# A hand-written engine order over five sub-layer boundaries, and adaLN weights loaded and multiplied in pairs

## The chip, the core and the metric

The kernel runs on one core of a Trainium2 chip. The metric is the device time of one launch, in microseconds (us). Engines are called TensorE (PE in the rows, PEld for its weight loads), VectorE (DVE), ScalarE (ACT), GpSimd (POOL) and SyncE (SP, whose queue issues nearly all DMAs).

## The reference, cut to what matters

Two layers of a hybrid trunk, for 128 context tokens (sample 0) and 128 latent tokens (sample 1), with the same weights and D = 1024. Everything is float32.

```python
def _layer(x, cond, st, l, p, alpha):
    ada = (silu(cond) @ p['w_ada'][l] + p['b_ada'][l]).reshape(..., 9, 1, D_MODEL)
    sh1, sc1, g1, sh2, sc2, g2, sh3, sc3, g3 = [ada[:, j] for j in range(9)]
    f1 = swiglu(x * (1 + sc1) + sh1, ffn1_w_gate, ffn1_w_up, ffn1_w_down)   # 1024 -> 2816 -> 1024
    x = layer_norm(alpha * x + 0.5 * g1 * f1, ...)
    y, new_st = mixer(x * (1 + sc2) + sh2, st, l, p)                        # GLA and mLSTM, merged
    x = layer_norm(alpha * x + g2 * y, ...)
    f2 = swiglu(x * (1 + sc3) + sh3, ffn2_w_gate, ffn2_w_up, ffn2_w_down)
    x = layer_norm(alpha * x + 0.5 * g3 * f2, ...)
```

So there are six sub-layers (FFN, mixer, FFN, twice) and five boundaries between them. At a boundary the LayerNorm of one sub-layer has to finish before the first product of the next can start.

## The kernel before, in words

Each weight matrix is cut into blocks of 512 output columns, and a block into units of up to four 128-row tiles. `load` fetches a unit from HBM in halves (`raw`, 512 KB, six buffers in `raw_p`), and `split_w` splits each half into a high part on ScalarE (`hi`, L304) and a low part on VectorE (`lo`, L305), seven buffers each. `consume(s, u)` multiplies unit u for sample s: per 128-row tile three matmuls, L320 (high x high), L321 and L322 (the cross terms), into the accumulator `acc0` or `acc1`. The main loop at the end of `hybrid_step` walks over all units: it consumes unit i for sample 0 and unit i-2 for sample 1 (LAG = 2).

The modulation values (adaLN) come from 9216 further weight columns a layer. `ada_unit(grp, k)` does one 128-row tile of two 1024-column pieces: two DMAs of 512 KB (`araw`), and four matmuls L168, each with 32 columns of weights in a column strip of its own of the array (`tile_position`), 512 moving columns and float32 operands; the profile has two records for each of these matmuls, since a float32 product takes two passes. 64 such products (the adaLN products of this text) are spread over the sub-layers by the list `due`; in the before version their weights come through `raw_p`.

At a boundary `ln_half` (VectorE: L378 or L380, L381, L382) takes half a row of the last product, `ln_finish` aggregates (L393), gets the reciprocal root through GpSimd (L386, L387), normalises `y` (L399), and `modulate` transposes it (L349, tile `xT`), applies scale and shift alternately on VectorE (L353) and ScalarE (L355) out of one PSUM bank, and splits the features into `xh` (ScalarE, L331) and `xl` (VectorE, L333). `residuals` then forms the next `x` (L420, L421).

In the mixers, `gates` and `chain` compute running maxima `Gr`, write them to DRAM (`Gd`, L589), and `rows_load` reads them back broadcast to all partitions (`Db`, L598); `decays` uses them on VectorE (L610).

What sets the order: a tile scheduler orders the instructions of every engine ahead of time from priorities, dependences and expected times; each engine then runs its list in order. Inside a `tc.manual_schedule` block the listed engines keep the order of the code. SP's queue also runs in order: an issue that waits holds up those behind it.

Of the kernel before, what the change touches and what calls it, by code (L numbers as in the profile page):

```python
# [28 lines left out]
LAG = 2  # L29
SLOTS = 21  # L30
PRIO = 100
# [3 lines left out]
def hybrid_step(ctx: ExitStack, tc: tile.TileContext, I, O, n_sub=6):  # L35
# [120 lines left out]
    def ada_unit(grp, k):  # L156

        raw = []
        for l, v in grp:
            r = raw_p.tile([128, 2, 512], F32, name="araw", tag="raw")  # L160
            nc.sync.dma_start(r.rearrange("p q n -> p (q n)"),
                              I["w_ada"][l, 128 * k:128 * (k + 1), 1024 * v:1024 * v + 1024])
            raw += [r[:, 0, :], r[:, 1, :]]
        if k == 0:
# [105 lines left out]
    class Block:  # L270
        def __init__(self, nk, srcs, x, post, pre=None):
            self.nk, self.srcs, self.x, self.post, self.pre = nk, srcs, x, post, pre
            self.acc = {}
# [11 lines left out]
    def load(u, part=None):  # L285
        b, k0, n, w, _ = u
        for h in range(0, n, 2):
            if part == 1:
                raw = w.pop("raw")
                split_w(raw, w, h)  # L290
                continue
# [4 lines left out]
            if part == 0:  # L296
                w["raw"] = raw
# [3 lines left out]
    def split_w(raw, w, h):  # L301
# [3 lines left out]
        V.tensor_tensor(lo, raw, hi.bitcast(F32), ALU.subtract)  # L305
# [3 lines left out]
    def consume(s, u):  # L309
        b, k0, n, w, _ = u  # L310
        if k0 == 0:
# [4 lines left out]
        for j in range(n):  # L316
# [6 lines left out]
        if k0 + n == b.nk:  # L323
            b.post(s, b.acc.pop(s))
# [13 lines left out]
    def modulate(s, xn, l, sub):  # L338
# [3 lines left out]
        xl[s] = s4("xl", [KT, 128], F32R)  # L342
        for g in range(2):
            mod_tiles(s, xn, l, sub, range(4 * g, 4 * g + 4))

    def mod_tiles(s, xn, l, sub, ks):
        pt = ms("xT", [4, 128])
        for j, k in enumerate(ks):
            T.transpose(pt[:, j, :], xn[:, 128 * k:128 * (k + 1)], ident)  # L349
        for j, k in enumerate(ks):  # L350
            gm_, bm_ = modF[:, l, sub, s, 0, k:k + 1], modF[:, l, sub, s, 1, k:k + 1]
            if j % 2 == 0:
                V.tensor_scalar(mf[s][:, k, :], pt[:, j, :], gm_, bm_, ALU.mult, ALU.add)  # L353
            else:
                A.activation(mf[s][:, k, :], pt[:, j, :], AF.Identity, scale=gm_, bias=bm_)  # L355
        sl = slice(ks[0], ks[-1] + 1)
        g = int(ks[0] > 0 and len(ks) == 4)
        fin["A", s, g], fin["V", s, g] = split_fm(xh[s][:, sl, :], xl[s][:, sl, :], mf[s][:, sl, :])

    gbc, lnbc, yt, bst, fin = {}, {}, {}, {}, {}  # L360
# [29 lines left out]
    def ln_finish(s, l, sub):  # L390
# [5 lines left out]
        if idx + 1 < n_sub:  # L396
            for n in range(2):
                sl = slice(512 * n, 512 * n + 512)
                V.tensor_scalar(y[:, sl], y[:, sl], mv[:, 0:1], r, ALU.subtract, ALU.mult)  # L399
        if idx + 1 < n_sub:  # L400
            l2, sub2 = divmod(idx + 1, 3)
            modulate(s, y, l2, sub2)
            later.append([3, s, y, lnbc["g"], lnbc["b"], fin["V", s, 1]])
# [9 lines left out]
    def residuals():  # L413

        for e in later:
            e[0] -= 1
        while later and later[0][0] <= 0:
            _, s, y, g, b, behind = later.pop(0)
            with tc.issue_after(behind):
# [4 lines left out]
    def ffn(l, sub, wg, wu, wd):  # L424
# [43 lines left out]
        def down_post(n):  # L468
            def f(s, acc):
                with tc.high_priority(offset=PRIO):  # L470
                    ln_half(s, n, acc, 0.5)
                    if n == 1:
                        ln_finish(s, l, sub)
# [7 lines left out]
    def mixer(l):  # L481
# [60 lines left out]
        def chain():  # L542
# [9 lines left out]
            tables = tc.keep_in_program_order(A.preload_act_table_set("natural_log_exp_and_others"))  # L552
            with tc.issue_after(tables.ins):
                A.activation(e, e, AF.Exp, scale=-1.0)
# [368 lines left out]
        b0 = units[first][0]  # L923
        pre0 = b0.pre

        def first_pre(s):
            gates(s)
            if pre0 is not None:
                pre0(s)

        b0.pre = first_pre
# [33 lines left out]
        def out_post(n):  # L965
            def f(s, acc):
                with tc.high_priority(offset=PRIO):
                    ln_half(s, n, acc, 1.0)
                    if n == 1:
                        ln_finish(s, l, 1)  # L970
# [28 lines left out]
    due = []  # L999
    for p in range(6):  # L1000
        c, m = sum(u[4] == p for u in units), len(jobs[p])
        first = 8 if p == 0 else 0
        e = c - first - (6 if p % 3 != 1 else 8)
        done = 0
        for j in range(c):
            upto = m * max(0, min(j + 1 - first, e)) // e
            due.append(jobs[p][done:upto])
            done = upto
# [52 lines left out]

    for i in range(s0, n + LAG):
        ahead = units[i + 1] if i + 1 < n else None
        if ahead and not last(i - LAG):
            load(ahead)
        if i < n:
# [3 lines left out]
        if ahead and last(i - LAG):  # L1072
            with tc.issue_after(fin["V", 0, 0]), tc.issue_after(fin["A", 0, 0]):
                load(ahead)
        residuals()
        if i < n:
            for a in due[i]:
                ada_unit(*a)

# [86 lines left out]
```

## Time and profile before

| | |
|---|---|
| median of 3 runs | 1611.5 us (1609.59 to 1613.73) |
| the profiled execution's own time | 1617.74 us |
| its span in the trace | 1615.9 us |
| TensorE busy | 1576.5 us (98%) |
| VectorE busy | 985.8 us (61%) |
| ScalarE busy | 757.1 us (47%) |
| mean granted TensorE clock | 0.992 |
| DMA | 350.19 MB, mean 217 GB/s |

Busy time of TensorE counts overlapping records once, so 98% does not say that each product ran at its best pace; for that the distance from the start of one matmul to the start of the next has to be read. The five boundaries lie at about 250, 628 to 648, 838, 1034 and 1405 to 1426 us.

### The profile page before, as it was taken

The numbers are of one execution on the slowest core, as the hardware profiler recorded it, in microseconds if no ns is written. First come the engines' busy times: TensorE is split into PE (matmuls) and PEld (weight loads), VectorE is DVE, ScalarE is ACT, GpSimd is POOL, SyncE is SP. The second block draws the span as 40 slices with busy tenths as digits, with TensorE's granted clock in tenths as the row PEclk, the third lists the DMA queues.
The fourth block names the chain that finished last, engine by engine and source line by source line (L and its number), as shares of the span: only waits on it lengthen the run. The fifth ranks groups of instructions, "written<-read, shape, count | busy, mean of one in ns | idle before, by whom it ended". The sixth has DMA issues, their size and how long they took to land.

```text
span 1615.9 us, 20299 instructions
## 1 busy us (share of the span) xinstructions
PE 1576.5 (98%) x7323; PEld 1190.9 (74%) x7323; DVE 985.8 (61%) x1627; ACT 757.1 (47%) x1096; POOL 55.6 (3%) x102
## 2 busy tenths in 40 slices
PE   7999999999999999999999999999999999999997
PEld 3676677777777777777778878777777777777886
DVE  3544458666776568554566555775677665765555
ACT  2443334646556434444344444454755563444441
POOL 2000001000000000000000000100000000000000
PEclk9999999999999999999999999999999999999999
DMA  9777976666766776666865657665665767646661
GB/s 329 271 265 251 312 230 220 220 221 203 253 216 213 256 265 187 195 222 215 278 186 161 181 180 254 193 197 192 187 215 165 260 209 242 214 143 183 182 235 65
DMA packets 195981, 350.19 MB, mean 217 GB/s; under 512 B 17516, under 2 KB 73596, under 8 KB 195880
## 3 DMA queue, kind: packets, MB, share of 16 engines
q1 hardware_dynamic: 195320, 348.68, 66.7%
q8 instruction: 58, 0.95, 0.2%
q0 software_dynamic: 384, 0.13, 0.1%
q14 instruction: 43, 0.35, 0.1%
q10 hardware_dynamic: 176, 0.07, 0.0%
HBM read 341.30 MB, written 7.54 MB: 216 GB/s over the span
## 4 chain that ended last, share of the span: by engine, by line
PE 81%; issue 8%; DVE 5%; DMA 2%; ACT 2%; POOL 1%; SPq 0%; DVEq 0%; POOLq 0%; ACTq 0%
PE acc L320 23%; PE acc L322 22%; PE acc L321 22%; PE adaps L168 3%; DVE lo L305 2%; DMA araw<-in_w_ada 1%; PE hT L433 1%; PE num L837 1%; ACT hi L304 1%; PE num L834 1%; PE gps L531 1%; PE zps L630 0%; DMA Db<-Gd 0%; PE rg L814 0%; PE gla_o L728 0%
## 5 line engine op out<-in xcount | busy, mean ns | idle before, releaser
L305 DVE TENSOR_TENSOR lo<-raw,hi 128x1024 fp32r<-128x1024 f32 x456 | 557.0, 1223 | 355.6 <-ACT hi L304 347.3
L304 ACT ACTIVATE hi<-raw 128x1024 fp32r<-128x1024 f32 x456 | 481.6, 1059 | 413.5 <-PE acc L322 389.3
L320 PE MATMUL acc<-hi,xh 128*128 128x512 f32 x1280 | 516.5, 405 | 7.5 <-ACT xh L331 6.3
L321 PE MATMUL acc<-lo,xh 128*128 128x512 f32 x1280 | 513.1, 401 | 4.3 <-DVE lo L305 4.3
L322 PE MATMUL acc<-hi,xl 128*128 128x512 f32 x1280 | 514.1, 402 | 0.1
L320 PEld LDWEIGHTS acc<-hi,xh 128*128 128x128 f32 x1280 | 241.9, 189 | 105.0 <-issue 27.3
L321 PEld LDWEIGHTS acc<-lo,xh 128*128 128x128 f32 x1280 | 241.9, 189 | 60.4 <-DVE lo L305 9.0
L322 PEld LDWEIGHTS acc<-hi,xl 128*128 128x128 f32 x1280 | 242.3, 189 | 57.4 <-issue 4.2
L320 PE MATMUL acc<-hi,hid 128*128 128x512 f32 x320 | 126.8, 396 | 0.0
L321 PE MATMUL acc<-lo,hid 128*128 128x512 f32 x320 | 126.7, 396 | 0.0
L322 PE MATMUL acc<-hi,hid 128*128 128x512 f32 x320 | 126.4, 395 | 0.0
L168 PE MATMUL adaps<-araw,condp 128*32 128x512 f32 x512 | 74.2, 605 | 0.7 <-DMA araw<-in_w_ada 0.7
L320 PEld LDWEIGHTS acc<-hi,hid 128*128 128x128 f32 x320 | 60.1, 188 | 18.8 <-issue 4.2
L321 PEld LDWEIGHTS acc<-lo,hid 128*128 128x128 f32 x320 | 60.1, 188 | 14.4 <-issue 0.8
L322 PEld LDWEIGHTS acc<-hi,hid 128*128 128x128 f32 x320 | 60.1, 188 | 13.7
L331 ACT ACTIVATE hid<-hT 128x512 fp32r<-128x512 f32 x40 | 23.8, 597 | 82.5 <-PE hT L433 82.5
L321 PE MATMUL acc<-lo,oh 128*128 128x512 f32 x128 | 51.3, 401 | 0.0
L320 PE MATMUL acc<-hi,oh 128*128 128x512 f32 x128 | 51.1, 399 | 0.0
L322 PE MATMUL acc<-hi,ol 128*128 128x512 f32 x128 | 50.6, 395 | 0.0
L440 ACT ACTIVATE sg<-acc 128x512 f32<-128x512 f32 x40 | 23.8, 598 | 45.7 <-PE acc L322 45.7
L333 DVE TENSOR_TENSOR hid<-hT,hid 128x512 fp32r<-128x512 f32 x40 | 27.5, 691 | 28.0 <-ACT hid L331 28.0
L387 POOL TENSOR_TENSOR rstd<-rstd,mhalf 128x1 f32<-128x1 f32 x12 | 13.1, 1094 | 814.8 <-DVE rstd L386 800.7
(246 smaller groups left out, 1481.8 us busy)
## 6 DMA issues: line engine op xcount, KB each, us to landing
araw<-in_w_ada SPq DMA_DIRECT2D x128, 512.0 KB
raw<-in_w_in SPq DMA_DIRECT2D x96, 512.0 KB
raw<-in_ffn_w_down SPq DMA_DIRECT2D x88, 512.0 KB
raw<-in_ffn_w_gate SPq DMA_DIRECT2D x80, 512.0 KB
raw<-in_ffn_w_up SPq DMA_DIRECT2D x80, 512.0 KB
raw<-in_w_in SPq DMA_DIRECT2D x96, 256.0 KB
araw<-in_w_ada SPq DMA_DIRECT2D x32, 256.0 KB
raw<-in_w_br_gla SPq DMA_DIRECT2D x16, 512.0 KB
```

The lines of the kernel that those rows point to most:

```text
L168: T.matmul(ps[32 * q:32 * q + 32, :], lhsT=condp[:, k, :], rhs=raw[q], start=(k == 0), stop=(k == KT - 1), tile_position=(0, 32 * q))
L304: A.activation(hi, raw, AF.Copy)
L305: V.tensor_tensor(lo, raw, hi.bitcast(F32), ALU.subtract)
L320: T.matmul(acc, lhsT=xh, rhs=wh, start=(k == 0), stop=False)
L321: T.matmul(acc, lhsT=xh, rhs=wl, start=False, stop=False)
L322: T.matmul(acc, lhsT=xl, rhs=wh, start=False, stop=(k == b.nk - 1))
L331: a = A.activation(dst_h, src, AF.Copy, scale=scale)
L333: v = V.tensor_tensor(dst_l, src, dst_h.bitcast(F32), ALU.subtract)
L433: T.transpose(pt[:, t, :], h[:, 128 * t:128 * (t + 1)], ident)
L440: A.activation(sg[s], acc, AF.Silu)
L531: T.matmul(ps[0:48, :], lhsT=wgt[:, k, :], rhs=mf[s][:, k, :], start=(k == 0), stop=(k == KT - 1))
L834: T.matmul(num, lhsT=sT[:, d, :], rhs=vh, start=True, stop=(s == 0))
```

## The change

Five things change.

1. A function `boundary(e)` replaces three turns of the main loop at each of the five boundaries and writes the order of VectorE, ScalarE and TensorE down: the next three units are loaded, their halves split at fixed places, sample 1's two late units are consumed while sample 0 is normalised, and sample 0's next two units before sample 1's transposes.
2. Two adaLN products (`fill`) of the following sub-layer stand in that order ahead of sample 1's transposes; the last boundary has none, since no products are left for the last sub-layer.
3. `modulate` uses two PSUM banks, VectorE reads the first and ScalarE the second, and the second half of `y` is normalised on ScalarE.
4. The other adaLN products are spread anew over the sub-layers. In the FFNs they are placed two at a time and their weights go to the `s4` pool; in the mixers they are placed singly and stay in `raw_p`.
5. The short unit of a 22-tile block comes first instead of last, `gates` runs in the second block of a mixer instead of the first, and the priorities of the LayerNorm code go.

```diff
-    def ada_unit(grp, k):
-        raw = []
+    def ada_load(grp, k, own):
+        raw = ada_w[grp, k] = []
         for l, v in grp:
-            r = raw_p.tile([128, 2, 512], F32, name="araw", tag="raw")
+            if own:
+                r = s4("araw", [2, 512])
+            else:
+                r = raw_p.tile([128, 2, 512], F32, name="araw", tag="raw")
...
-            n = min(step, b.nk - k0)
+            n = (b.nk - k0) % step or step
...
+        for k in range(4):
+            V.tensor_scalar(mf[s][:, k, :], pts[0][:, k, :], *gb(k), ALU.mult, ALU.add)
+        for k in range(4, 8):
+            if k == 6:
+                split_fm(xh[s][:, 0:4, :], xl[s][:, 0:4, :], mf[s][:, 0:4, :])
+                between()
+            gm_, bm_ = gb(k)
+            A.activation(mf[s][:, k, :], pts[1][:, k - 4, :], AF.Identity, scale=gm_, bias=bm_)
+        split_fm(xh[s][:, 4:8, :], xl[s][:, 4:8, :], mf[s][:, 4:8, :])
...
-        b0.pre = first_pre
+        units[first + 3][0].mid = gates
...
     jobs = [adas(((0, 2), (0, 5)), ((0, 3), (0, 4))),
-            adas(((0, 6), (0, 7)), ((0, 8), (1, 2)), ((1, 0), (1, 1))),
-            adas(((1, 3), (1, 4))),
-            [],
-            adas(((1, 5), (1, 8)), ((1, 6), (1, 7))),
+            adas(((0, 6), (0, 7))),
+            adas(((0, 8), (1, 2)), ((1, 0), (1, 1))),
+            adas(((1, 3), (1, 4)), ((1, 5), (1, 8))),
+            adas(((1, 6), (1, 7))),
             []]
...
+        step = 2 if p % 3 != 1 else 1
+        todo = jobs[p][0 if p == 0 else 2:]
...
+    def boundary(e):
+        u, u1, u2, u3 = units[e:e + 4]
+        fill = jobs[u1[4]][:2]
+        load(u1, 0)
+        load(u2, 0)
+        for a in fill:
+            ada_load(*a, True)
+        load(u3, 0)
+        with tc.manual_schedule(engines={V.engine, A.engine, T.engine}):
...
+            split_half(u1, 0)
+            consume(0, u)
+            half0 = consume(1, units[e - 2], defer=True)
+            split_half(u1, 2)
+            apply, features = steps.pop(0)
+            apply()
+            consume(1, units[e - 1])
+            features(lambda: split_half(u2, 0))
+            split_half(u2, 2)
+            half0()
+            consume(1, u)
+            split_half(u3, 0)
+            consume(0, u1)
+            consume(0, u2)
+            apply, features = steps.pop(1)
+            apply()
+            split_half(u3, 2)
+            for a in fill:
+                ada_unit(*a)
+            consume(0, u3, 0, 2)
+            features(lambda: None)
+            consume(0, u3, 2)
```

The rows below are those of the compiled programs. Lines move: L168 becomes L175 in the changed kernel, L320 to L322 become L332 to L334, L305 becomes L311, L378 to L382 become L404 to L408, L399 becomes L428 and L429, and L598 becomes L625.

**adaLN products on TensorE, second FFN of layer 0.** Before, one product between units of the gate block:

```order
L321 MATMUL acc1_5753<-lo_5594,xh_5509 128x512
L322 MATMUL acc1_5753<-hi_5593,xl_5510 128x512
L168 MATMUL adaps_5638<-araw_5766,condp_97 32x512 x2
L168 MATMUL adaps_5638<-araw_5768,condp_97 32x512 x2
L320 MATMUL acc0_5740<-hi_5730,xh_5393 128x512
L321 MATMUL acc0_5740<-lo_5731,xh_5393 128x512
```

In the changed kernel, the first product of a pair late in the same FFN (araw_6418 and araw_6420 are its two weight tiles; a row without a count is one matmul):

```order
L175 MATMUL adaps_6032<-araw_6418,condp_97 32x512
L463 MATMUL hT_6465<-ident_93,sg_6462 128x128 x2
L175 MATMUL adaps_6032<-araw_6418,condp_97 32x512
L333 MATMUL acc0_6398<-lo_6429,hid_5668 128x512
L334 MATMUL acc0_6398<-hi_6428,hid_5668 128x512
L175 MATMUL adaps_6032<-araw_6420,condp_97 32x512 x2
L332 MATMUL acc0_6398<-hi_6434,hid_5862 128x512
L333 MATMUL acc0_6398<-lo_6435,hid_5862 128x512
```

The four matmuls of a product stood in one group; here they stand in groups of 1, 1 and 2 with other matmuls between them, and the second product of the pair follows in two groups of 2. In the whole order before, the 256 adaLN matmuls stand in 69 groups of at most four; in the changed order they stand in 73: 15 of eight, 4 of five, and 54 of at most four. By sub-layer the groups go from 19, 26, 8, 0, 16, 0 to 19 (5 of them long), 11 (1), 16 (6), 16 (6), 11 (1), 0.

**The end of the mixer of layer 0 on VectorE, sample 1.** Before (y_5429 is sample 1's row, y_5293 sample 0's, acc1_5345 and acc1_5459 are its two halves):

```order
L378 TENSOR_TENSOR y_5429<-acc1_5459,gbc_5254 128x512
L382 BN_STATS bst_5430<-y_5429 128x6
L381 SCALAR_TENSOR_TENSOR y_5429<-x1_132,y_5429 128x512
L305 TENSOR_TENSOR lo_5536<-raw_5533,hi_5535 128x1024
L382 BN_STATS bst_5430<-y_5429 128x6
L305 TENSOR_TENSOR lo_5542<-raw_5539,hi_5541 128x1024
L393 BN_AGGR mv_5501<-bst_5430 128x2
L420 TENSOR_TENSOR x0_131<-y_5293,lngbc_5141 128x1024
L386 TENSOR_SCALAR rstd_5503<-mv_5501 128x1
L305 TENSOR_TENSOR lo_5550<-raw_5547,hi_5549 128x1024
L399 TENSOR_SCALAR y_5429<-y_5429,mv_5501,rstd_5503 128x512 x2
L421 TENSOR_TENSOR x0_131<-x0_131,lnbbc_5142 128x1024
```

In the changed kernel (y_5311 is sample 1's row, acc1_5185 and acc1_5265 its two halves, lo_5337 and lo_5372 the two halves of the third unit of the next sub-layer):

```order
L404 TENSOR_TENSOR y_5311<-acc1_5185,gbc_5094 128x512
L407 SCALAR_TENSOR_TENSOR y_5311<-x1_132,y_5311 128x512
L408 BN_STATS bst_5312<-y_5311 128x6
L404 TENSOR_TENSOR y_5311<-acc1_5265,gbc_5094 128x512
L407 SCALAR_TENSOR_TENSOR y_5311<-x1_132,y_5311 128x512
L408 BN_STATS bst_5312<-y_5311 128x6
L419 BN_AGGR mv_5331<-bst_5312 128x2
L412 TENSOR_SCALAR rstd_5333<-mv_5331 128x1
L311 TENSOR_TENSOR lo_5337<-raw_5214,hi_5336 128x1024
L427 SCALAR_TENSOR_TENSOR nm_5367<-mv_5331,rstd_5333 128x1
L429 TENSOR_SCALAR y_5311<-y_5311,mv_5331,rstd_5333 128x512
L311 TENSOR_TENSOR lo_5372<-raw_5216,hi_5371 128x1024
```

The first half of sample 1's row stood apart from the second, interleaved with it and with features of sample 0; now all of sample 1's row stands in one piece, behind the last feature and weight split of sample 0's side, and the split lo_5372 stands between `y` and sample 1's features, which follow it.

**The maxima of the first mixer, on SP's queue.** Before, from the row behind the write of `Gd` to the first read of `Db` (raw and araw are weights):

```order
L294 DMA raw_2450<-in_w_in 128x2x512
L591 DMA out_m<-mt_2161 1x4
L592 DMA out_m<-mt_2161 1x4
L294 DMA raw_2456<-in_w_in 128x2x512
L161 DMA araw_2533<-in_w_ada 128x1024
L161 DMA araw_2535<-in_w_ada 128x1024
L294 DMA raw_2541<-in_w_in 128x2x256 x2
L294 DMA raw_2548<-in_w_in 128x2x256 x2
L294 DMA raw_2657<-in_w_in 128x2x256 x2
L294 DMA raw_2664<-in_w_in 128x2x256 x2
L161 DMA araw_2742<-in_w_ada 128x1024
L598 DMA Db_2462<-Gd_2166 128x512
```

In the changed kernel:

```order
L300 DMA raw_2878<-in_w_in 128x2x512
L300 DMA raw_2965<-in_w_in 128x2x512
L616 DMA Gd_2436<-mc_2125 128x128
L618 DMA out_m<-mt_2431 1x4
L619 DMA out_m<-mt_2431 1x4
L625 DMA Db_2469<-Gd_2436 128x512 x2
L300 DMA raw_2971<-in_w_in 128x2x512
L300 DMA raw_3076<-in_w_in 128x2x512
```

Eleven rows of other issues, with their waits, stood between the write and the read; now only the two `out_m` writes stand between them. On VectorE, the first instruction that uses `Db` stood 30 rows behind the last of `Gr`, and now stands six behind it:

```order
L606 TENSOR_SCALAR mc_2125<-pp1_119,m0col0_122 32x128 x4
L612 TENSOR_TENSOR mt_2431<-cumS_2410,GT_2429 128x8 x2
L311 TENSOR_TENSOR lo_2750<-raw_2747,hi_2749 128x1024
L663 SCALAR_TENSOR_TENSOR ela_2488<-zps_2485,ela_2488 128x512
L311 TENSOR_TENSOR lo_2875<-raw_2872,hi_2874 128x1024
L354 TENSOR_TENSOR lal_2494<-ela_2488,lah_2493 128x512
L637 SCALAR_TENSOR_TENSOR Db_2469<-Db_2469,gpad_116,mk_2123 128x128 x8
L684 COPY qk_2589<-qkT_2584 128x256
```

After those eight rows come the key and query products of the GLA part (`qk`, `E`, `kL`), for which TensorE waits.

## Rows read from the trace of the kernel before

**Rows 1.** The page, busy time and share of the span:

```profile
PE 1576.5 (98%) x7323; PEld 1190.9 (74%) x7323; DVE 985.8 (61%) x1627; ACT 757.1 (47%) x1096; POOL 55.6 (3%) x102
```

**Rows 2.** The page, the chain that ended last, by engine:

```profile
PE 81%; issue 8%; DVE 5%; DMA 2%; ACT 2%; POOL 1%; SPq 0%; DVEq 0%; POOLq 0%; ACTq 0%
```

**Rows 3.** Waits of TensorE: total us, times, longest us.

```profile
PE acc L320 <- ACT xh L331: 6.3, 3, 2.3
...
PE acc L321 <- DVE lo L305: 4.3, 6, 1.0
PE xT L349 <- DVE y L399: 3.5, 7, 0.9
...
PE gla_o L728 <- DVE attT L725: 2.6, 2, 2.5
```

**Rows 4.** Timeline of TensorE around one adaLN product: start us, us, instruction.

```profile
85.52 0.39 PE L321 MATMUL acc<-lo,xh 128*128 128x512 f32 x1
85.75 0.39 PE L322 MATMUL acc<-hi,xl 128*128 128x512 f32 x1
86.07 1.07 PE L168 MATMUL adaps<-araw,condp 128*32 128x512 f32 x8
87.07 0.50 PE L320 MATMUL acc<-hi,xh 128*128 128x512 f32 x1
87.40 0.39 PE L321 MATMUL acc<-lo,xh 128*128 128x512 f32 x1
```

**Rows 5.** The same around parts of products, one matmul and then two.

```profile
64.08 1.04 PE L168 MATMUL adaps<-araw,condp 128*32 128x512 f32 x2
65.06 0.50 PE L321 MATMUL acc<-lo,xh 128*128 128x512 f32 x1
...
152.66 1.05 PE L168 MATMUL adaps<-araw,condp 128*32 128x512 f32 x4
153.64 0.50 PE L320 MATMUL acc<-hi,xh 128*128 128x512 f32 x1
```

**Rows 6.** The second passes of the product of Rows 4.

```profile
86.53 0.61 PE L168 MATMUL adaps<-araw,condp 128*32 128x512 f32 x4
```

**Rows 7.** Timeline of TensorE, boundary after the first mixer.

```profile
645.43 0.40 PE L322 MATMUL acc<-hi,xl 128*128 128x512 f32 x1
648.15 0.50 PE L320 MATMUL acc<-hi,xh 128*128 128x512 f32 x1 [2.32 <-ACT xh L331]
```

**Rows 8.** Windows of TensorE: us, busy (instructions), granted clock, DMA share, GB/s.

```profile
648.00:655.00 7.00, 6.85 (x23) 0.76 0.06 8
842.00:850.00 8.00, 7.79 (x28) 0.79 0.46 132
1426.00:1434.00 8.00, 7.92 (x28) 0.79 0.18 48
1097.00:1105.00 8.00, 8.00 (x25) 0.64 0.39 125
```

**Rows 9.** Timeline of VectorE, end of the first mixer, sample 0.

```profile
623.55 0.69 DVE L378 TENSOR_TENSOR y<-acc,gbc 128x512 f32<-128x512 f32 x1 [0.46 <-PE acc L322]
...
625.97 0.15 DVE L386 TENSOR_SCALAR rstd<-mv 128x1 f32<-128x1 f32 x1
626.05 1.23 DVE L305 TENSOR_TENSOR lo<-raw,hi 128x1024 fp32r<-128x1024 f32 x1
627.72 0.55 DVE L399 TENSOR_SCALAR y<-y,mv,rstd 128x512 f32<-128x512 f32 x1 [0.44 <-POOL rstd L387]
```

**Rows 10.** Issue of `Db` on SP and first use on VectorE, both mixers.

```profile
303.30 0.42 SPq L598 DMA_DIRECT2D Db<-Gd  x1
310.36 0.88 DVE L610 SCALAR_TENSOR_TENSOR Db<-Db,gpad,mk 128x128 f32<-128x128 f32 x3 [3.06 <-DMA Db<-Gd]
...
1087.34 0.94 SPq L598 DMA_DIRECT2D Db<-Gd  x2
1095.12 0.35 DVE L610 SCALAR_TENSOR_TENSOR Db<-Db,gpad,mk 128x128 f32<-128x128 f32 x1 [2.67 <-DMA Db<-Gd]
```

More of the change, by code (lines that the diff above doesn't have):

```diff
@@ L315, in consume @@
         acc = b.acc[s]
-        for j in range(n):
+        for j in range(j0, n if j1 is None else j1):
             k = k0 + j
@@ L336, in split_fm, with modulate @@
         return a.ins, v.ins
-    def modulate(s, xn, l, sub):
+    def modulate(s, xn, l, sub, between):
         mf[s] = s4("mf", [KT, 128])
@@ L342, in modulate, with gb @@
         xl[s] = s4("xl", [KT, 128], F32R)
+        pts = []
         for g in range(2):
[L344 to L360, printed above, removed]
+            pt = ms("xT", [4, 128])
+            pts.append(pt)
+            for j in range(4):
+                k = 4 * g + j
+                T.transpose(pt[:, j, :], xn[:, 128 * k:128 * (k + 1)], ident)
+        def gb(k):
+            return modF[:, l, sub, s, 0, k:k + 1], modF[:, l, sub, s, 1, k:k + 1]
+        for k in range(4):
[7 more added lines that the diff above has]
+        split_fm(xh[s][:, 4:8, :], xl[s][:, 4:8, :], mf[s][:, 4:8, :])
+    gbc, lnbc, yt, bst, fin, steps = {}, {}, {}, {}, {}, {}
     def ln_prefetch(s, l, sub):
@@ L396, in ln_finish, with apply, features @@
         if idx + 1 < n_sub:
[L397 to L400, printed above, removed]
             l2, sub2 = divmod(idx + 1, 3)
-            modulate(s, y, l2, sub2)
-            later.append([3, s, y, lnbc["g"], lnbc["b"], fin["V", s, 1]])
+            def apply():
+                nm = sm("nm", 1)
+                V.scalar_tensor_tensor(nm, mv[:, 0:1], -1.0, r, ALU.mult, ALU.mult)
+                A.activation(y[:, 512:], y[:, 512:], AF.Identity, scale=r, bias=nm)
+                V.tensor_scalar(y[:, :512], y[:, :512], mv[:, 0:1], r, ALU.subtract, ALU.mult)
+            def features(between):
+                modulate(s, y, l2, sub2, between)
+                later.append([s, y, lnbc["g"], lnbc["b"]])
+            steps[s] = apply, features
         else:
@@ L413, in residuals @@
     def residuals():
[L415 to L419, printed above, removed]
+        while later:
+            s, y, g, b = later.pop(0)
+            with tc.issue_after(fin["lo"]):
                 V.tensor_tensor(x[s], y, g, ALU.mult)
@@ L469, in f @@
             def f(s, acc):
[L470 to L473, printed above, removed]
+                ln_half(s, n, acc, 0.5)
+                if n == 1:
+                    ln_finish(s, l, sub)
             return f
@@ L551, in chain @@
             A.activation(e, zf, AF.Abs)
[L552 to L554 removed]
+            A.activation(e, e, AF.Exp, scale=-1.0)
             A.activation(e, e, AF.Ln, bias=1.0)
@@ L993, in hybrid_step @@
     jobs = [adas(((0, 2), (0, 5)), ((0, 3), (0, 4))),
-            adas(((0, 6), (0, 7)), ((0, 8), (1, 2)), ((1, 0), (1, 1))),
-            adas(((1, 3), (1, 4))),
-            [],
-            adas(((1, 5), (1, 8)), ((1, 6), (1, 7))),
+            adas(((0, 6), (0, 7))),
+            adas(((0, 8), (1, 2)), ((1, 0), (1, 1))),
+            adas(((1, 3), (1, 4)), ((1, 5), (1, 8))),
+            adas(((1, 6), (1, 7))),
             []]
-    due = []
+    due_load, due = [], []
     for p in range(6):
[L1001 to L1008, printed above, removed]
+        c = sum(u[4] == p for u in units)
+        step = 2 if p % 3 != 1 else 1
+        todo = jobs[p][0 if p == 0 else 2:]
+        first = 9 if p == 0 else 5
+        places = c - first - (7 if p % 3 != 1 else 10)
+        groups = [todo[a:a + step] for a in range(0, len(todo), step)]
+        at = [first + places * a // max(1, len(groups)) for a in range(len(groups))]
+        ld, mm = [[] for _ in range(c)], [[] for _ in range(c)]
+        for a, g in zip(at, groups):
+            ld[a - 1] += g
+            mm[a] += g
+        due_load += ld
+        due += mm
     for t in range(2):
@@ L1060, in last @@
         return 0 <= i < n and (i == n - 1 or units[i + 1][4] != units[i][4])
[L1064 to L1068, printed above, removed]
+    def boundary(e):
[7 more added lines that the diff above has]
+        with tc.manual_schedule(engines={V.engine, A.engine, T.engine}):
+            if u1[4] % 3 > 0:
+                tables = ("natural_log_exp_and_others", "silu_and_others")[u1[4] % 3 - 1]
+                tc.keep_in_program_order(A.preload_act_table_set(tables))
+            split_half(u1, 0)
[20 more added lines that the diff above has]
+            consume(0, u3, 2)
+    i = s0
+    while i < n + LAG:
+        if i + 1 < n and last(i):
+            boundary(i)
+            i += 3
+            continue
+        if i + 1 < n:
+            load(units[i + 1])
+        if i < n and not last(i - 3):
             consume(0, units[i])
@@ L1071, in hybrid_step @@
             consume(1, units[i - LAG])
[L1072 to L1075, printed above, removed]
+        if i - s0 > 2 and last(i - 5):
+            residuals()
         if i < n:
+            for a in due_load[i]:
+                ada_load(*a, units[i][4] % 3 != 1)
             for a in due[i]:
                 ada_unit(*a)
+        i += 1
 def _consts():
```

46 lines of the change are left out of this document (26 added, 20 removed).

## The prediction

> **What bounds the kernel now.** I read the busy table first: TensorE is busy for 98% of the span, VectorE 61%, ScalarE 47% [rows 1]. The chain that ended last says the same, 81% of it is TensorE, with 8% of issue and 5% of VectorE [rows 2]. So two things can change the time: how long TensorE takes over its own instructions, and how long it stands still. The list of TensorE's waits gives the second: for the features `xh` 6.3 us, for the normalised row `y` 3.5 us, for a split weight 4.3 us (of which about 1 at boundaries, the rest at the start of the kernel), and for one GLA product 2.6 us [rows 3]. The timeline shows the shape of the worst: at the boundary behind the first mixer the next start comes 2.72 us after the last, 2.32 of it waiting for sample 1's `xh` [rows 7]. Then I read windows just behind such waits, because a wait may go on costing: the granted clock is 0.76 over 7 us there and 0.79 over 8 us behind two other boundaries, where waits of the same kind stood [rows 8]; the mean over the run is 0.992. At half speed for part of a window the loss is one minus the mean clock, so 7 x 0.24 = 1.7, 8 x 0.21 = 1.7 and 1.7 us.
>
> All five boundaries together thus lose 6.3 + 3.5 + 1 = 10.8 us of waiting, 5.1 us of slow clock, and some 2 us more because a wait of 2.32 us made 2.72 - 0.23 = 2.49 us of gap, 0.17 more, in about a dozen places. That is 18 us, 1.1% of the time: the most that a better boundary can give back.
>
> **The adaLN products, the largest term.** The boundary gets the attention in the change, but the products between units are moved too, and TensorE pays for each group of them. One product between ordinary matmuls: starts at 85.52, 85.75, 86.07, 87.07 and 87.40 [rows 4]. An ordinary matmul starts 0.23 after the one before it, so entering costs 0.32 - 0.23 = 0.09, the product 1.00, leaving 0.33 - 0.23 = 0.10: 1.19 us. Now the parts that a few products were already cut into: two of the four matmuls take 0.98 from start to next start, and a single one takes 0.98 as well [rows 5]. The time of a group is therefore not its number of matmuls. Its four matmuls run side by side in four column strips, and what takes the time is the two passes of any one of them: the second passes start 0.46 after the first [rows 6]. A product cut in two costs twice 1.17.
>
> A group of more than four uses a strip again and has four passes in a row: 3 x 0.46 + 0.54 = 1.92, with entry and exit 2.11, against 2.38 for two products apart. So a pair kept whole saves 0.27, and a pair cut into four groups costs 2.3 more. The order of the changed program has 54 groups of at most four and 19 longer ones, where 69 stood. Before: 69 x 1.19 = 82.1 us. After: 54 x 1.19 + 19 x 2.11 = 64.3 + 40.1 = 104.4. That is +22 us, all of it on TensorE, which sets the end. No trace row shows a group of eight, so I bound it: from below by 1.19 + 0.46 = 1.65 (only one further pass shows), giving 64.3 + 31.4 - 82.1 = +14; from above by two separate products, 2.38, giving +27. I take 2.11, since the passes of one strip followed each other at 0.46 in the rows.
>
> By sub-layer this says where to look: +4 in the first FFN, -17 in the first mixer (26 groups to 11), +15 in the second FFN, +24 in the third, -5 in the second mixer, 0 in the last.
>
> The Trainium skill's page "TensorEngine Tiling (Array Packing)", section Key Properties, puts the cost elsewhere: changing the tiling mode drains the engine, while the tiles themselves run independently. By that alone the count of groups, 69 against 73, would matter and this term would be about +1 us. The rows of a single matmul at 0.98 speak against it as the whole story.
>
> **The boundary.** I count from T, the issue of sample 0's last product, with durations from the first mixer's end. TensorE has 24 matmuls of sample 1 at 0.23 (5.6), sample 0's transposes (0.9), 12 more (to 9.3), 24 for sample 0 (to 14.9), the two filling products (2.1, to 17.0), 6 more (to 18.4), then sample 1's transposes. VectorE for sample 0: it starts at about T + 0.3 and needs 2.4 from the first row operation to the root's input, and the root is back 1.75 later (623.55, 625.97, 627.72) [rows 9]; with `y` the row is ready at 5.2 to 5.4, before 5.6: no wait, where up to 0.9 stood [rows 3]. A weight split of 1.2 us lies inside the root's time and costs nothing.
>
> Then VectorE works through features and splits until about 12.5. In the three boundaries behind an FFN sample 1 needs 2.4, the root 1.75 and `y` 0.6: ready at about 17.3, ahead of 18.4; the features after it come 0.3 to 0.8 late. Behind a mixer both halves of sample 1's row are queued there, 2.2 us more: ready at 19.5, 1.1 late, and the split queued between `y` and the features (1.06 on ScalarE, then 1.2 on VectorE) makes TensorE wait another 1.9. That is 3 us behind the first mixer. Behind the second there is no filling product, so TensorE arrives 2.1 earlier: 5 us, and about 1 us of clock as before. Sum after: 0.3 + 3 + 0.8 + 0.3 + 5 + 1 = 10.4, against 18: -8 us. Bounds: -16 if the estimates of lateness are all a microsecond or two too high, -2 if the waits behind mixers are each doubled. Other covers: the residual update moves later, behind VectorE's idle time, at no cost; the short unit first and `gates` later add no instruction to TensorE.
>
> **The maxima in the mixers.** The read of `Db` took 7.1 us to its first use in the first mixer and 7.8 in the second, and in the second VectorE stood 2.67 us there with the GLA masks queued behind [rows 10], so that TensorE waited 2.5 [rows 3] and then ran at a clock of 0.64 for 8 us [rows 8], 2.9 us lost; with a microsecond in the first mixer, 6.5 in all. Now write and read are adjacent on SP, and the first use comes six rows behind the maxima. TensorE has 30 ordinary matmuls (7.0), one adaLN group (1.2) and short products, which I take at 3: about 11 us before it needs what VectorE makes behind `Db`, 3.4 us after the data are there. Its wait is then the landing of the write plus 7.4 + 3.4 - 11, about the landing itself. No row shows it: not below 0, not above a read of 7.8. I take 4 in the middle, less what hides, 3.4 and 0.5 of clock, in both mixers: 7.8 against 6.5, +1 us, bounds -6 and +14.
>
> **Sum.** +22 - 8 + 1 = +15 us. Against the profiled execution's own 1617.7 (1615.9 of span): 1632.7. That execution stood 6.2 above the median of 1611.5, so the forecast for the median is 1626 us. I call 0.3%, 4.8 us, no change: about what such a measurement can tell.
>
> **Rivals.** *Parts overlap their neighbours, so that only switches cost* (the faster side). Place: each adaLN group. If the fixed part, 0.19 + 0.14, is all that another group costs, the term is 4 x 0.33 = +1.3, and the sum 1.3 - 8 + 1 = -6: 1606. For it: the four strips do overlap each other. Against it: the parts in the rows took 0.98 with ordinary matmuls on both sides. It decides when the term falls below +2 us. Chance 0.10. The Trainium skill's rule on draining, named above, would have it so. *Long groups are cheap*: at 1.65 the term is +14, and with a boundary that gains 14 the sum is near zero, 1608 to 1616. Chance 0.14. *The read of `Db` becomes the new stall*: if the write lands as slowly as a read, 7.8, both mixers stand about 7 us and lose 2 to 3 to the clock: 14 us instead of 1, giving 1639. For it: the same queue, 512 KB weights ahead of it. Against it: the write is small. Chance 0.13. *The pairs don't come out as pairs* is no rival but the forecast: of the products outside the boundaries few stand as eight.
>
> **Numbers.** The forecast has 0.63, its own range 1617 to 1636. To leave out no more than 2 in 10 the range takes most of the cheap case and part of the stall: 1610 to 1638. Faster 0.10, same 0.14, slower 0.76.
>
> **What would show it.** Right: in the profile after, groups of two adaLN matmuls still take 0.98 and groups of eight 1.8 to 2.0; the first mixer is shorter by some 16 us and the second and third FFN longer by 10 and 20; waits for `xh` fall below 3 us in all behind FFNs, but a wait for `y` of 1 to 3 us stands at both mixer ends, with the slow clock behind the second. Wrong: if the third FFN is not over 15 us longer, the largest term fails; if the waits at boundaries don't fall, the boundary term does.

## The result and the profile after

The changed kernel takes 1636.5 us (median of 4 runs, 1634.0 to 1636.6) against 1611.6 (4 runs, 1609.6 to 1613.7): a ratio of 1.015, 95% interval 1.0133 to 1.0168. It is slower by 24.8 us, inside the range of 1610 to 1638 by 1.5 us and 10 us above the forecast of 1626. Its profiled execution took 1636.6, with 1634.8 of span.

The page, busy time and then the chain that ended last, against [rows 1, 2]:

```profile
PE 1596.8 (98%) x7323; PEld 1193.1 (73%) x7323; DVE 986.6 (60%) x1627; ACT 764.3 (47%) x1106; POOL 58.2 (4%) x102
...
PE 84%; DVE 5%; DMA 4%; issue 3%; ACT 3%; POOL 1%; SPq 0%; DVEq 0%; POOLq 0%; ACTq 0%
```

TensorE has as many instructions as before and 20.3 us more of busy time, while its span grew by 18.9; VectorE has 0.8 more. So the added time is not idle time of TensorE. The waits of TensorE, against [rows 3]:

```profile
PE acc L333 <- DVE lo L311: 9.0, 9, 3.3
...
PE adaps L175 <- DMA araw<-in_w_ada: 3.3, 6, 1.2
...
PE acc L332 <- ACT xh L352: 0.6, 2, 0.3
```

The waits for `xh` have fallen from 6.3 to 0.6 and those for `y` are gone; more is waited for a split weight `lo` (9.0 against 4.3) and for adaLN weights. Where the busy time went, the timeline of TensorE tells: first a product cut into pieces in the third FFN, then a pair that stayed whole, and a group of five matmuls (two records each, so ten), against [rows 4 to 6]:

```profile
1001.51 1.05 PE L175 MATMUL adaps<-araw,condp 128*32 128x512 f32 x2
1002.49 0.50 PE L333 MATMUL acc<-lo,hid 128*128 128x512 f32 x1
...
1003.15 1.05 PE L175 MATMUL adaps<-araw,condp 128*32 128x512 f32 x4
1004.14 0.50 PE L332 MATMUL acc<-hi,hid 128*128 128x512 f32 x1
...
656.38 0.40 PE L334 MATMUL acc<-hi,xl 128*128 128x512 f32 x1
656.71 1.92 PE L175 MATMUL adaps<-araw,condp 128*32 128x512 f32 x16
658.57 0.50 PE L332 MATMUL acc<-hi,xh 128*128 128x512 f32 x1
658.90 0.39 PE L333 MATMUL acc<-lo,xh 128*128 128x512 f32 x1
...
181.02 1.90 PE L175 MATMUL adaps<-araw,condp 128*32 128x512 f32 x10
182.85 0.66 PE L463 MATMUL hT<-ident,sg 128*128 128x128 f32 x4
```

From start to next start: one matmul 0.98, two 0.99, eight 1.86, five 1.83. The starts around the group of eight are 0.33 apart on both sides, where ordinary matmuls are 0.23 apart, so entry and exit cost some 0.2 there as in [rows 4]. Summed from start to next start over the whole trace, adaLN groups take 110.0 us, against 85.7 before; in both sums the products of the kernel's start are counted too (L244, 17.7, and L237 before, 16.0), which the change does not touch. By sub-layer (from sample 0's first `xT` to the next, both profiled executions, all in us):

| | FFN 1 | mixer 1 | FFN 2 | FFN 3 | mixer 2 | last FFN |
|---|---|---|---|---|---|---|
| before | 250.0 | 378.4 | 210.0 | 196.1 | 371.9 | 209.6 |
| after | 251.3 | 366.8 | 219.9 | 221.7 | 366.6 | 208.7 |
| difference | +1.3 | -11.7 | +9.8 | +25.7 | -5.3 | -0.9 |
| of it adaLN groups | +5.0 | -14.3 | +13.4 | +24.4 | -4.2 | 0 |

In the first column 1.7 of the +5.0 belong to the products of the kernel's start. In the new order 15 `acc` matmuls (3.5 us) that stood ahead of a mixer's first transposes stand behind them: they moved from FFN to mixer in this table, once for each mixer.

The same 18.9 us split by kind of matmul, each from its start to the next start over the whole trace: adaLN groups +24.3, `acc` products with their waits and slow clock -10.4, the short products (transposes and the mixers' small matmuls) +5.0.

The worst boundary is now the one behind the second mixer. TensorE there, then VectorE, against [rows 7, 9]:

```profile
1435.41 0.40 PE L332 MATMUL acc<-hi,xh 128*128 128x512 f32 x1
1439.10 0.79 PE L333 MATMUL acc<-lo,xh 128*128 128x512 f32 x1 [3.29 <-DVE lo L311]
1439.69 0.63 PE L334 MATMUL acc<-hi,xl 128*128 128x512 f32 x1
```

```profile
1433.28 0.68 DVE L404 TENSOR_TENSOR y<-acc,gbc 128x512 f32<-128x512 f32 x1
...
1437.74 0.15 DVE L412 TENSOR_SCALAR rstd<-mv 128x1 f32<-128x1 f32 x1
1437.82 1.23 DVE L311 TENSOR_TENSOR lo<-raw,hi 128x1024 fp32r<-128x1024 f32 x1
```

TensorE waits for a split that VectorE has queued behind 4.5 us of row operations for both halves of sample 1. The granted clock over that stretch, against [rows 8]:

```profile
1436.00:1444.00 8.00, 4.90 (x16) 4.12 (x17) 6.05 (x11) 3.57 (x6) 1.48 (x1) 0.61 0.33 95
```

No other boundary shows a slow clock in this profile. `Db` in the first mixer, issue on SP and first use, against [rows 10]:

```profile
326.56 0.83 SPq L625 DMA_DIRECT2D Db<-Gd  x2
...
330.43 1.14 DVE L637 SCALAR_TENSOR_TENSOR Db<-Db,gpad,mk 128x128 f32<-128x128 f32 x4 [0.53 <-DMA Db<-Gd]
```

3.9 us instead of 7.1. TensorE has no wait for `attT` any more, which cost it 2.6 us before [rows 3].

### The profile page after: what moved, and what is told of

Same layout as the page of the kernel before. It is cut to its first block, busy times and chain, and to the rows that moved or that the text cites. A ratio compares the mean times of both kernels' runs of the same rounds, so it can differ in the third digit from the quotient of the medians.

```text
span 1634.8 us, 20313 instructions
## 1 busy us (share of the span) xinstructions
PE 1596.8 (98%) x7323; PEld 1193.1 (73%) x7323; DVE 986.6 (60%) x1627; ACT 764.3 (47%) x1106; POOL 58.2 (4%) x102
## 4 chain that ended last, share of the span: by engine, by line
PE 84%; DVE 5%; DMA 4%; issue 3%; ACT 3%; POOL 1%; SPq 0%; DVEq 0%; POOLq 0%; ACTq 0%
PE acc L332 23%; PE acc L333 23%; PE acc L334 23%; PE adaps L175 5%; DMA araw<-in_w_ada 4%; DVE lo L311 2%; PE hT L463 1%; ACT hi L310 1%; PE num L864 1%; POOL rstd L413 1%; PE num L861 1%; PE oT L799 1%; PE gps L560 0%; PE sfin L770 0%; PE rg L841 0%
## 5 line engine op out<-in xcount | busy, mean ns | idle before, releaser
L311 DVE TENSOR_TENSOR lo<-raw,hi 128x1024 fp32r<-128x1024 f32 x456 | 556.3, 1223 | 381.4 <-ACT hi L310 369.5
L332 PE MATMUL acc<-hi,xh 128*128 128x512 f32 x1280 | 514.0, 403 | 2.5 <-ACT hi L310 1.0
L334 PE MATMUL acc<-hi,xl 128*128 128x512 f32 x1280 | 509.5, 399 | 0.0
L332 PEld LDWEIGHTS acc<-hi,xh 128*128 128x128 f32 x1280 | 240.9, 188 | 91.4 <-issue 21.7
L334 PEld LDWEIGHTS acc<-hi,xl 128*128 128x128 f32 x1280 | 241.2, 188 | 55.5 <-issue 3.7
L332 PE MATMUL acc<-hi,hid 128*128 128x512 f32 x320 | 126.5, 397 | 0.0
L334 PE MATMUL acc<-hi,hid 128*128 128x512 f32 x320 | 126.0, 394 | 0.0
L175 PE MATMUL adaps<-araw,condp 128*32 128x512 f32 x512 | 96.6, 602 | 3.5 <-DMA araw<-in_w_ada 3.3
L332 PEld LDWEIGHTS acc<-hi,hid 128*128 128x128 f32 x320 | 60.1, 188 | 17.2 <-issue 1.7
L334 PEld LDWEIGHTS acc<-hi,hid 128*128 128x128 f32 x320 | 60.1, 188 | 13.8
L334 PE MATMUL acc<-hi,ol 128*128 128x512 f32 x128 | 50.7, 396 | 0.0
L332 PE MATMUL acc<-hi,oh 128*128 128x512 f32 x128 | 50.6, 395 | 0.0
L175 PEld LDWEIGHTS adaps<-araw,condp 128*32 128x32 f32 x512 | 16.0, 108 | 40.8 <-issue 29.2
```

Source lines behind the costliest of these rows:

```text
L311: fin["lo"] = V.tensor_tensor(lo, raw, hi.bitcast(F32), ALU.subtract).ins
L332: T.matmul(acc, lhsT=xh, rhs=wh, start=(k == 0), stop=False)
L334: T.matmul(acc, lhsT=xl, rhs=wh, start=False, stop=(k == b.nk - 1))
```

## The experiments

Theory: the slowdown is the groups, which cost their longest strip whatever they hold, and which the compiled order cuts. The rivals: groups cost only entry and exit; or the boundary and the gates made the loss. All times are medians; "before" was 1611.5, 1611.1, 1611.0 and 1609.7 in the four sets, so times of different sets compare to no better than some 2 us. A ratio is to "before" of the same set, with its 95% interval.

**Strips reversed.** The last-loaded strip first, so that all four strips are ready when the first is:

```
-        for q in range(4):
+        for q in (3, 2, 1, 0):
             T.matmul(ps[32 * q:32 * q + 32, :], lhsT=condp[:, k, :], rhs=raw[q],
```

> The changed kernel, in which each adaLN product takes its four column strips in the order 3, 2, 1, 0 instead of 0, 1, 2, 3, so that the strip whose weights are loaded last comes first and the compiled order no longer cuts a product or a pair: 54 groups (40 of four matmuls, 14 of eight, those of the kernel's start included) instead of 77 (54 of at most five, counted with entry and exit at 1.17 us, where 23 are longer or end a pair, 2.05 each). Theory (a group costs its longest strip, however few matmuls it has): 40 x 1.17 + 14 x 2.05 = 75.5 us instead of 106.8, so 31 us less than the changed kernel: 1605 us, 0.4% under the kernel before. Rival (only entry and exit cost, 0.33 for each of 23 groups): 8 us less, 1629 us. Rival (the boundary's order or the mixers' new order made the 25 us): no more than 5 us less, over 1631 us. If waiting for the last-loaded strip stalls TensorE, waits of adaps for araw grow beyond the 3.3 us of the changed kernel and take back as much.

Measured 1605.0, ratio to before 0.9966 (0.9955 to 0.9978): the forecast of the theory, with both rivals 24 us away or more. The adaLN rows of the listing by line, of the changed kernel and then of this one (busy us, mean ns of a record; idle before):

```profile
L175 PE MATMUL adaps<-araw,condp 128*32 128x512 f32 x512 | 96.6, 602 | 3.5 <-DMA araw<-in_w_ada 3.3
```

```profile
L175 PE MATMUL adaps<-araw,condp 128*32 128x512 f32 x512 | 65.3, 602 | 2.5 <-DMA araw<-in_w_ada 2.5
```

The same 512 records of the same mean length are busy for 31.3 us less, because more of them lie side by side; the time fell by 31.5. From start to next start the adaLN groups take 78.2 instead of 110.0. The trace has 36 groups of four and 14 of eight besides the kernel's start, and they take the same 1.00 and 1.85 as whole groups of the changed kernel without a wait inside, so it is the number of groups that fell and not the price of one. Waiting for the last strip costs nothing more (2.5 of waits).

**Reversed, products one by one** (`step = 1`).

> As the run with the strips reversed, but the products of the FFNs stand one by one instead of in pairs: 64 groups, 60 of four matmuls and 4 of eight. Theory: 60 x 1.17 + 4 x 2.05 = 78.4 us, 28 less than the changed kernel, 1608 us: whole pairs are worth only 3 us against whole singles. Rival (only entry and exit cost): 13 groups fewer than the changed kernel, 4 us less, 1632 us.

Measured 1606.7, 0.9971 (0.9960 to 0.9981). Ten groups more than the run before and 1.7 us, which is within the noise: a whole pair is hardly better than two whole products. What cost the time was the cutting.

**Loaded earlier, strips in order** (`ld[a - 2]` for `ld[a - 1]`, bounded at a sub-layer's start).

> The changed kernel with the strips in their order 0 to 3, but each adaLN weight outside the boundaries loaded one unit earlier. The compiled order then has 55 groups (19 of eight, 6 of five, 30 of at most four). Theory: 30 x 1.17 + 25 x 2.05 = 86.3 us, 20 less than the changed kernel: 1616 us. Rival (only entry and exit cost): 22 groups fewer, 7 us less, 1629 us. Rival (boundary or mixers): 1631 or more.

Measured 1610.9, 0.9998 (0.9989 to 1.0007): 25.6 us faster than the changed kernel where 20 were expected. Its adaLN rows:

```profile
L175 PE MATMUL adaps<-araw,condp 128*32 128x512 f32 x512 | 75.5, 601 | 0.0
```

Busy adaLN time is 21.1 less, and the waits for `araw` in these products are 0.0 against 3.3. Groups and those waits together give 24.

**The kernel before, once more.**

> The kernel before, unchanged, for a second profile: its first profiled execution stood 6 us above the median of its runs. If the stall of VectorE at Db in the second mixer (2.67 us) with the slow clock behind it (0.64 over 8 us) belongs to that execution, it is missing here and the span is some 4 to 6 us shorter; if it is in every execution, it stands here again.

One execution, 1614.0 with 1612.2 of span. The waits of TensorE are nearly the same (`xh` 6.3, `y` 3.7, `attT` 2.1), and VectorE waits 5.9 us for `Db` (6.5 in the first profile), so that stall is the kernel's own. What is missing is slow clock. The windows of [rows 8] at 842 and 1097, in this execution:

```profile
842.00:850.00 8.00, 7.78 (x39) 6.17 (x38) 7.45 (x12) 3.43 (x6) 1.46 (x1) 1.00 0.46 134
1097.00:1105.00 8.00, 8.00 (x33) 6.32 (x32) 3.12 (x6) 5.86 (x8) 0.00 (x0) 0.89 0.32 102
```

The granted clock is 1.00 there instead of 0.79, and 0.89 instead of 0.64 behind the stall at `Db`. Windows of 8 us below 0.97 lose 5.4 us over the run without its start and its last window, in the first profile 8.5.

**Reversed, gates in the first block**, where the kernel before has them (`first_pre` calls the gates and then the block's own `pre`).

```
-        units[first + 3][0].mid = gates
+        b0 = units[first][0]
+        b0.pre = first_pre
```

> The run with the strips reversed (1605.0 us), and besides the mixer's gates back in its first block, where the kernel before has them. In the compiled order each of the four chunk updates of a mixer then has acc matmuls between kmT and cfin again (in the reversed run two of four stand bare: kmT, then eight cfin rows with nothing between). Theory (the bare updates cost the mixers their gain: short products and their waits take 75.5 us in each mixer of the reversed run against 70.4 and 71.1 in the kernel before): 5 us less in each mixer, 1595 us, if the read of Db stays hidden. If the stall of VectorE at Db comes back with the gates' old place (5.9 us in the kernel before, with its slow clock 6.5 for the span), 1601 us. Rival (the gates' place is worth nothing either way): 1605 us.

Measured 1618.6, 1.0042 (1.0027 to 1.0058): 13.6 us slower than with the gates in the fourth unit, against the theory, its variant and the rival. TensorE at the start of the first mixer:

```profile
249.74 0.60 PE L560 MATMUL gps<-mf,wgt 128*48 128x128 f32 x4
256.84 0.47 PE L565 MATMUL gpT<-ident,ag 128*128 128x128 f32 x1 [6.51 <-DVE ag L563]
256.97 0.78 PE L332 MATMUL acc<-hi,xh 128*128 128x512 f32 x1
```

The transposition of the gates waits for two copies on VectorE, which stand behind splits and sample 1's row in the boundary's fixed order; the granted clock is 0.59 from 256 to 264. The second mixer has the same wait, 6.50. So the new boundary needs the later place of the gates.

**The changed kernel, gates in the first block.**

> The changed kernel, strips in order 0 to 3, with the gates alone back in the first block. Its compiled order has 71 adaLN groups instead of 77, which by the theory of groups is worth 99.8 - 106.8 = -7 us, and no bare chunk update: short products 73.1 to about 70.5 in each mixer, -5 us. Together 1624 us; with the stall at Db back 1631 us. Rival (the gates' place is worth nothing): 1636 us.

Measured 1642.9, 1.0194 (1.0178 to 1.0211). The same waits (13.4 us for `gpT`) outweigh the 6 groups that it saves. So the gates' move does not cause the slowdown; it holds it down.

**The kernel before with whole pairs**, the distribution of the change (jobs, steps and places, but no fill), reversed strips, boundary and gates untouched.

```
-            for a in due[i]:
+            for a in due_load[i]:
+                ada_load(*a, units[i][4] % 3 != 1)
+            for a in due[i]:
```

> The kernel before, boundary code and gates untouched, with the change's distribution of adaLN products alone: the same pairs, loaded a unit ahead, strips reversed so that they stay whole, and nothing kept for the boundaries: 58 groups, 76.7 us by the theory of groups. Against the kernel before: 76.7 - 85.4 = -9 us, and one nearly bare chunk update in each mixer, +2 each: 1607 us. Against the reversed run with the gates in the first block the difference is the boundary: theory 8 us more in the FFN sub-layers and the last (waits for xh and y and slow clocks of the old boundary). Rival (the new boundary is worth nothing): the FFN sub-layers, counted without their adaLN groups, take as long as in the run with the new boundary.

Measured 1609.1, 0.9983 (0.9975 to 0.9992). The reversed run with the new boundary is 4.1 us faster, 1.2 of which the groups explain: boundary and gates together are worth some 3 us, hardly clear of the noise (0.9975 to 0.9992 touches 0.9955 to 0.9978). The two profiles say what lies under it: in the reversed run with the new boundary the `acc` products with their waits and slow clock take 12.1 us less, and the short products 8.4 more, nearly all of it in the mixers (75.6 us each against 71.8 and 71.0). The FFN sub-layers and the last, without their adaLN groups and the `acc` matmuls that moved, are 5.5 us shorter with it, 1.6 of which is slow clock at the kernel's start. So by these two profiles the new boundary is worth something, and much of it is lost again in the mixers.

**Reversed, no filling products.**

> The run with the strips reversed, but without the two adaLN products at each of the four boundaries that have them; they stand in the sub-layer instead (56 groups, 77.8 us instead of 75.5). Theory (they cover sample 1's wait, which then shows: 2.05 us at each, less a slack of up to 1): 4 to 8 us of new waits for split weights or y at the boundaries, 1611 to 1615 us. Rival (they cover nothing, sample 1's row is in time without them): 1607 us.

Measured 1620.9, 1.0060 (1.0045 to 1.0075): 15.9 us slower, more than the theory had. Waits for `lo` grow from 9.0 to 13.8, and a new one of 2.7 us stands in each mixer (`argA` for `lal`); slow clock costs 10.2 us by 8 us windows without the kernel's start and end, against 2.6 in the reversed run. The filling products cover real waits, and the slow clock adds to the price of those that show without them. Why the wait of `argA` comes with their absence was not shown.

**Reversed, chunk updates covered.** In the reversed run two of four chunk updates of each mixer stand bare on TensorE:

```profile
407.13 0.38 PE L880 MATMUL kmT<-ident,yh 128*128 128x128 f32 x2
408.50 1.57 PE L889 MATMUL cfin<-vm,kw 128*128 128x257 f32 x6 [0.98 <-ACT kw L882]
410.68 0.70 PE L889 MATMUL cfin<-vm,kw 128*128 128x257 f32 x2 [0.62 <-DVE nf L891]
```

Pairs in the mixers and an earlier end of their products (`step = 2`, 14 for 10) put `acc` matmuls between them again.

> The run with the strips reversed (1605.0 us; gates in the fourth unit, boundaries as in the changed kernel), with the mixers' adaLN products in pairs too and their last one four units earlier. In the compiled order no chunk update is bare any more (three to five acc matmuls between kmT and cfin in all eight), and there are 48 adaLN groups (28 of four, 20 of eight, 73.8 us instead of 75.5). Theory (the bare updates are what the mixers lost): kmT and cfin rows together from 12.6 to about 7 us in each mixer as in the kernel before, 5 us less in each, so 1605 - 10 - 2 = 1593 us. Rival (the time of a mixer is set elsewhere, by VectorE's chain from gate to gate, and a covered update only moves the wait): 1603 us, with the waits of cfin gone and others as long in their place.

Measured 1608.4 (1602.7 to 1611.3), 0.9981 (0.9970 to 0.9992). The theory failed and the rival held: the waits of `cfin` for `kw` fell from 3.9 to 0.6, but a wait of 3.10 for `yh` stands in each mixer instead, and in the profiles (here that of the fastest run, 1602.7) both mixers are as long as in the reversed run: 363.8 and 363.4 us against 363.7 and 363.8. TensorE's waits:

```profile
PE acc L333 <- DVE lo L311: 9.0, 9, 3.3
PE rg L841 <- DVE yh L837: 6.2, 2, 3.1
```

What sets the pace of the mixers' chunks stays open; its runs also spread over 8.6 us.

**Half a row earlier**, on top of that.

```
+            half0()
             features(lambda: split_half(u2, 0))
             split_half(u2, 2)
-            half0()
```

> The same kernel as the covered one, and at both mixer ends the row operations of sample 1's first half (2.06 us of VectorE) put ahead of sample 0's features instead of behind them. Theory (VectorE's queue is the bound at a mixer's end): sample 1's row comes 2 us earlier, so that the 3.3 us wait for lo behind the second mixer falls to about 1.3 and its slow clock with it; sample 0's features come 1.25 us later, of which up to 1 shows as a wait for xh: 1 to 3 us less in all. Rival (the features are the tighter): 1 to 3 us more.

Measured 1605.0, 0.9962 (0.9946 to 0.9977). The waits for `lo` fall from 9.0 to 6.3, the longest from 3.3 to 1.8, as expected; with the spread of the run that it builds on, the 3.3 us of difference are no firm number.

**The kernel before, strips reversed.**

> The kernel before with nothing but its adaLN strips in the order 3, 2, 1, 0. Its compiled order then has 69 groups instead of 73 (one product is still cut), 80.7 us instead of 85.4 by the theory of groups: 5 us less, 1606.5 us. Rival (only entry and exit cost): 4 x 0.33 = 1.3 us less, 1610 us.

Measured 1611.4, 0.9997 (0.9984 to 1.0009): a miss. Its adaLN rows are busy for 69.2 us (73.8 in the second profile of before), so the 4.6 are there, but the profiled execution loses as much elsewhere: up to the first boundary waits and slow clock cost 19.0 us where the second profile of before has 14.6, 3.4 of the difference being slow clock in the first 64 us, and in the first mixer TensorE waits 2.6 us at one place for a split weight `hi`. Whether the reversal or this execution did that was not told apart.

**The parts that gained, together**: reversed strips, FFN weights loaded a unit earlier, half a row earlier.

> The run with the strips reversed (1605.0 us), with the FFNs' adaLN weights loaded one unit earlier besides, and at the mixer ends the row operations of sample 1's first half ahead of sample 0's features. The compiled order has 43 adaLN groups (18 of four, 25 of eight), 72.3 us by the theory of groups instead of 75.5: 3 us less. The waits of adaps for araw (2.5 us in the reversed run) go, since the earlier loads had none: 2 us less. The wait for lo at the second mixer's end falls by 1.5 with part of its slow clock: 2 us less. Together 1598 us. Rival (the mixers, whose order is unchanged, and the start of the kernel, whose waits vary, hold the time): 1603 to 1605 us.

Measured 1598.6 (1595.9 to 1599.9), 0.9928 (0.9915 to 0.9942): as the theory had it, and faster than both kernels. Its adaLN rows:

```profile
L175 PE MATMUL adaps<-araw,condp 128*32 128x512 f32 x512 | 63.2, 600 | 0.1
```

The waits for `lo` are 7.0 us instead of 9.0, the longest 1.8 instead of 3.3. The mixers are as long as in the reversed run, so the gain is in the FFNs. What each of the two additions brought alone on top of the reversed run was not measured.

## Why the prediction was right, and where its size was off

**What bounds** was read rightly: TensorE's own instructions decide, and the waits moved by less than they did. The largest term and its place were right as well. That 1636.5 still lies in the range is in part luck: it is just above the forecast's own 1617 to 1636, in the 2 us that were added for a new stall at `Db`, which did not come.

**The adaLN groups** (+22, bounds +14 and +27): counted as in the prediction, from start to next start with 0.19 for entry and exit, these groups take 82.7 us before and 106.2 after, +23.4. The long group is 1.86 and 0.19, 2.05 where 2.11 was forecast. By sub-layer it is +3, -17, +15, +27, -5 and 0, for a forecast of +4, -17, +15, +24, -5 and 0. What the forecast lacked is that a pair can also wait inside: four of the fifteen groups of eight took 2.0, 2.2, 3.1 and 4.1, together 3.9 us over their 1.85, the two longest of them in the third FFN with waits for `araw` in them. Another 1.7 us is in the products of the kernel's start, which the change does not touch and the forecast did not count. The reversed run shows the cause: nothing but the cutting undone, and 31.5 us came back.

**The boundaries** (-8): counted as in the prediction, the gaps behind the five boundaries are 0.5, 3.3, 1.3, 0.6 and 6.5 us with the slow clock, 12.2 where 10.4 was forecast and 18 was counted before, so -6. The place of each was right and the wait's name wrong: no `y` is waited for, since the weight split that I had queued behind `y` is reached by TensorE first. The old boundary under the same products is only some 3 us slower, since that test counts the mixers' loss as well.

**`Db`** (+1): the stall is gone, and the new one of the forecast, 3.4 in each mixer, did not come: the read took 3.9 us and TensorE does not wait. What the mixers gained there they gave back in part at a place that the prediction put at nothing, the later gates. In the mixers the short products with their waits take 73.2 and 73.1 us instead of 70.4 and 71.8, the second of which had the old wait of 2.5 in it; the chunk updates, `kmT` and `cfin`, take 9.9 in each instead of 7.0, and 6.2 with the gates back in the first block. Without the adaLN groups and the 15 matmuls that moved into each, the two mixers together are 1.6 us shorter than in the first profile.

**The step that was off most** is the base. I took the sum against the profiled execution, 6.2 us above the median, and carried that surplus over to the kernel after. After, the profiled execution stands 0.1 above its median. The miss of 10 us is 6.1 from there, 1.4 from the adaLN groups, 1.7 from the kernel's start and 0.8 from boundaries and mixers; all four went the same way. None of the 72 timed runs of the kernel before was as long as its first profile (1606.6 to 1616.5, against 1617.7). The second profile says of what the surplus was made, as far as it goes: 3 us of slow clock, behind the wait at the boundary at 840 and behind the stall at `Db`, both of which the change removes or shrinks. A gain over such an accident is none over the median. The rest of the surplus stays open.

**Rivals.** That only switches cost is out: 23 groups fewer brought 31.5 us and not 8, and a group of eight takes 0.86 longer than one of four with no switch between. The Trainium skill's page "TensorEngine Tiling (Array Packing)", section Key Properties, has the drain at a change of mode and lets tiles run independently; the trace agrees with the second for up to four strips (0.98 to 1.00 for one to four matmuls) and bounds the first by the 0.19 of entry and exit. Cheap long groups (1.65) are out at 2.05, and `Db` did not stall.

**Of what was to show it**, the groups' lengths, the third FFN (+25.7), the second (+9.8) and the fall of `xh` came; the first mixer is shorter by 11.7 and not 16, and 3.5 of the difference is the shift of `acc` matmuls over its border; the wait at both mixer ends came, but for `lo` and not `y`, and the slow clock stood behind the second.

## What to carry to other kernels

Before moving work into pairs or bigger pieces, look at the compiled order for whether the pieces stay whole: a piece whose operands land one after the other is cut there, and the engine pays for each part. Issuing the part that depends on the last transfer first, one line, turned a loss of 25 us into a gain of 6. And take a second profile before adding up: what one execution lost to slow clock is no stock from which a change can draw.

## What the runs showed of the hardware

One to four column-strip matmuls in a group take 0.98 to 1.00 us whatever their number and order. A group of five takes as long as one of eight, 1.83 and 1.86 us: the fifth pays the whole second round. A wait of TensorE of 6.51 us left the granted clock at a mean of 0.59, between its two levels of 1.2 and 2.4 GHz, over the next 8 us, and one of 3.29 at 0.61 over the 8 us around it, so some 3 us more each. The same wait can be followed by slow clock in one execution and not in another: behind the 1.61 us for `xh` at 840 the granted clock was 0.79 over 8 us in the first profile of the kernel before and 1.00 in the second.
